# A hybrid attention block without the fifteen matrix products on a tile of ones ahead of its first data

## The chip, the cores and the metric

The kernel runs on one core of one Trainium2 chip. A core has a matrix engine (TensorE, PE in the profile, with its weight loads listed as PEld), a vector engine (VectorE, DVE), a scalar engine (ScalarE, ACT), GpSimd (POOL) and SyncE (SP), which here issues most of the DMAs. Each engine takes its own instructions in the order in which the program lists them, and waits for the others by semaphores. TensorE writes its results into PSUM, in banks of 512 float32 columns; the other operands lie in SBUF. The metric is the time of one execution on the device, in microseconds (us).

## The reference

The reference is one layer of a trunk with three groups of attention heads, on 512 tokens of width 1024, in float32. Cut to what matters here:

```python
hn = rms_norm(x, ln_mix)                 # per token
z  = hn @ w_in                           # 1024 x 3590, columns split among the head groups
# group A: 4 heads, difference of two softmax maps, ALiBi bias, norm per head
# group B: 6 heads, bias from a cumulative forget gate
# group C: 6 heads, clipped relative-position bias
# q and k of every head are normalised: q / sqrt(mean(q^2) + eps) * gain
h = x + concat(o_a, o_b, o_c) @ w_out
h = h + conv_gated_mlp(rms_norm(h, ln_ffn))        # width-3 causal convolution, 2816 hidden
h = h + (p @ w_ple_proj) * sigmoid(rms_norm(h, ln_ple) @ w_ple_gate)
```

The change concerns the very start: the first columns of `hn @ w_in`, the q, k and v of the first pair of group A.

## The kernel before, in words

Tokens are cut into four tiles of 128 (`NT`), the width of 1024 into eight slices of 128 (`KD`). To keep float32 accuracy at the faster matrix rate, each operand is split into a rounded high part and a low rest; a product is then three products, high by high, high by low and low by high (`mm3`). Split activations lie transposed in `Th` and `Tl`, and split weights are called `A_hi`/`A_lo`, `A_h`/`A_l` or `w_hi`/`w_lo` in the profile. ScalarE makes the high part (a cast), VectorE the low one (a subtraction).

The kernel begins with the loads. `load_k` (line 248) brings one slice of transposed x and one slice of the first weights for each of the eight slices k, nearly all on SyncE's queue; the weights of the second projection (`A0b_r`) and the four token tiles of x (`h`, by `load_x`, line 255) follow on the same queue. A few small loads go by ScalarE's and GpSimd's queues. These SyncE loads are kept in the order of the program.

Between the loads and the first products stands the part that the change touches. `wt` (line 100) is a tile of ones in a corner of `oall`, which later holds attention outputs. `warm(WARM)` (lines 269 and 297) makes 15 float32 products of 128 x 64 on it into a PSUM bank `wm` of the ring `t`, which has three banks; nothing reads the result.

`first_products` (line 299) follows. For each slice k it makes `th`, the weight split `wh`/`wl` and `tl`, and then 12 products: three combinations by four token tiles, accumulated in four PSUM banks `z0`, two from the ring `z` and two from the ring `s`. So 96 products of 128 x 384 make the first projection, and all four token tiles end together. x is not normalised before the product; the factor of each token, `rstd`, is applied afterwards. `stats` (line 293) has ScalarE square and sum each token tile of x (`n_sq`), and GpSimd makes 1/sqrt of it. Only behind these four stand, in ScalarE's order, the squares of the projection (`A_sq`), from which VectorE and GpSimd make the norm of each head (`A_rs`); then come the scaled q and k (`A_zn`) and v (`A_V`).

TensorE goes on with the second projection (`A0b_z`, three products per slice and token tile, into banks from the rings `t`, `o`, `t` and `s` for the four token tiles), with the transposes of the scaled q and k (`A_q_p`, `A_k_p`) set between them, and then with the projections of the following head pairs, among whose products the attention of the finished pairs is dealt out by a written table of slots. TensorE's order is pinned throughout; those of ScalarE and VectorE are pinned in the first projection and from the attention on. Later stages (output projection, gated MLP, gated embedding) follow a list of tasks with planned costs.

Of the kernel before, what the change touches and what calls it, by code (L numbers as in the profile page):

```python
# [15 lines left out]
P = 128  # L16
# [4 lines left out]
HD = 64  # L21
# [32 lines left out]
def kernel(ctx: ExitStack, tc: tile.TileContext, x, xt0, xt, pt_in, small, g_ffn_in, bias_c,  # L54
# [31 lines left out]
    pe, act, dve, pool, sp = (Engine(e) for e in (nc.tensor, nc.scalar, nc.vector, nc.gpsimd, nc.sync))  # L86

    def bank(tag, name):
        return ps.tile([P, 512], F32, tag=tag, bufs={"z": 2, "s": 2, "t": 3, "o": 1}[tag], name=name)
# [7 lines left out]
    ap = p1.__enter__()  # L97
    oall = ap.tile([P, 6, S], F32, tag="oall", name="oall")

    wt = oall[:, 4, P : 2 * P]  # L100
    dve.memset(wt, 1.0)
    nhalf = cp.tile([P, 8], F32, tag="nhalf", name="nhalf")
    dve.memset(nhalf, -0.5)
    onec = cp.tile([P, 1], F32, tag="onec", name="onec")
# [1 line left out]
    ident = cp.tile([P, P], F32, tag="ident", name="ident")  # L106
    make_identity(nc, ident)
    rstd = cp.tile([P, NT, 4], F32, tag="rstd", name="rstd")
    WARM = 15
    cols = cp.tile([P, 206], F32, tag="cols", name="cols")  # L110

    def col(c0, i=0):
# [151 lines left out]
    for t in range(3):  # L264
        load_x(t)
    pe.pinned = True
    wm = bank("t", "warm")

    def warm(n):
        for _ in range(n):  # L270
            pe.matmul(wm[:, 0:HD], wt, wt[:, 0:HD], start=True, stop=True)

    UP, DN = slice(0, HD), slice(HD, P)
    HALF = (UP, DN)

# [17 lines left out]
    def stats(t):  # L293
        token_stats(t, h[:, t, :], ap.tile([P, D], BF16, tag="e3", bufs=2, name=f"n1_sq{t}"))
        done("n", t)

    warm(WARM)
    z0 = [bank("zzss"[t], f"A0_z{t}") for t in range(NT)]
    def first_products():
        for k in range(KD):  # L300
# [503 lines left out]
    for j, (pr, part, *_) in enumerate(PARTS[1:], 1):  # L804
        n = w_in[j].shape[3]
# [824 lines left out]
    t = 0.0  # L1630
# [114 lines left out]
```

## Time and profile before

| | |
|---|---|
| median of 3 runs | 731.0 us (729.09 to 731.97) |
| profiled execution: span from first to last instruction | 728.0 us |
| profiled execution: total time beside the span | not given |
| TensorE busy | 709.6 us, 97% of the span |
| VectorE, ScalarE, GpSimd busy | 76%, 54%, 37% of the span |
| products on the tile of ones | from 1.04 us to the first data product at 7.47 us |

A row of a timeline gives the start in us from the beginning of the span, the length in us, the engine, the line, the operation, the tile written and the tiles read, shapes, and the number of instructions that were merged into the row. In square brackets stands the idle time of the engine just before it, and what ended that. All operations recorded through the kernel's helper carry its line, L78, so tiles tell more than lines. A float32 product appears as two records, so the 15 products on ones are 30. TensorE's matmuls overlap, so the rate is read from one start to the next, not from the length.

### The profile page before, as it was taken

The page shows a single profiled execution, that of the slowest core. Times are in us where ns is not written, and L with a number is a line of the kernel's source. Part 1 is how long each engine was busy: PE and PEld are TensorE (multiplying, and loading weights), DVE is VectorE, ACT ScalarE, POOL GpSimd, SP SyncE. Part 2 cuts the span into 40 slices and gives each one's busy share as a digit, 9 for nine tenths or more (in the row PEclk, how much of TensorE's full clock was granted, in tenths as well). Part 3 has the DMA queues.
Part 4 walks back from the last instruction along what each step waited for, and adds up shares of the span by engine and source line. Part 5 has one row for each costly group of instructions (what it writes and reads, how often), then busy time and mean ns, then how long its engine had stood idle before and what let it go on. Part 6 is the DMA issues. An engine that isn't in the chain of part 4 may idle for free. (4 is left out here: it accounts for less than half of the span.)

```text
span 728.0 us, 11909 instructions
## 1 busy us (share of the span) xinstructions
PE 709.6 (97%) x4234; PEld 637.8 (88%) x4234; DVE 555.8 (76%) x1091; ACT 393.8 (54%) x745; POOL 267.3 (37%) x355
## 2 busy tenths in 40 slices
PE   9998999999999999999999999999999999999997
PEld 9997989988999987889888899888998888899886
DVE  7678787887878854857878868787898779988552
ACT  6646775865766663554655544544445543544821
POOL 4585676766665640201201144020520004361400
PEclk9999999999999999999999999999999999999999
DMA  9453425413212125463444333562254322222441
GB/s 312 177 147 110 101 81 124 133 35 109 87 34 70 59 47 166 161 234 77 143 138 122 103 108 117 135 168 66 87 172 119 95 86 72 67 73 91 158 129 58
DMA packets 36950, 83.22 MB, mean 114 GB/s; under 512 B 4214, under 2 KB 6262, under 8 KB 36892
## 3 DMA queue, kind: packets, MB, share of 16 engines
q1 hardware_dynamic: 32844, 73.52, 31.7%
q0 software_dynamic: 3760, 8.66, 6.1%
q8 instruction: 33, 0.54, 0.3%
q10 hardware_dynamic: 288, 0.30, 0.1%
q14 instruction: 25, 0.20, 0.1%
HBM read 74.19 MB, written 4.21 MB: 108 GB/s over the span
## 5 line engine op out<-in xcount | busy, mean ns | idle before, releaser
L78 DVE TENSOR_TENSOR w_lo<-w_raw,w_hi 128x768 fp32r<-128x768 f32 (+1 forms) x118 | 113.9, 985 | 19.4 <-ACT w_hi L78 18.8
L78 ACT CAST w_hi<-w_raw 128x768 fp32r<-128x768 f32 (+1 forms) x118 | 89.6, 786 | 68.1 <-POOL w_raw L78 30.4
L78 PE MATMUL u<-Tl,w_hi 128*128 128x512 f32 (+1 forms) x336 | 125.5, 374 | 0.8 <-DVE Tl L78 0.8
L78 PE MATMUL u<-Th,w_hi 128*128 128x512 f32 (+1 forms) x336 | 125.6, 374 | 0.2 <-ACT pps L78 0.2
L78 PE MATMUL u<-Th,w_lo 128*128 128x512 f32 (+1 forms) x336 | 125.3, 373 | 0.0
L78 POOL TENSOR_TENSOR w_raw<-w_raw,w_raw 128x768 f32<-128x768 f32 (+1 forms) x30 | 54.2, 1828 | 146.9 <-DVE w_lo L78 115.4
L78 PEld LDWEIGHTS u<-Tl,w_hi 128*128 128x128 f32 x336 | 63.0, 188 | 13.0 <-DVE Tl L78 1.2
L78 PEld LDWEIGHTS u<-Th,w_hi 128*128 128x128 f32 x336 | 63.0, 188 | 12.6 <-ACT pps L78 0.7
L78 PEld LDWEIGHTS u<-Th,w_lo 128*128 128x128 f32 x336 | 63.0, 188 | 12.5
L78 DVE SCALAR_TENSOR_TENSOR c<-u,cols,c 128x511 f32<-128x511 f32 x76 | 56.7, 747 | 19.7 <-ACT c L78 18.4
L78 POOL DMA_DIRECT2D w_raw<-in_w_up_dram x9 | 7.9, 908 | 97.7 <-DMA w_raw<-in_w_up_dram 83.6
L78 ACT ACTIVATE c<-u,cols 128x512 f32<-128x512 f32 x38 | 29.5, 777 | 23.8 <-PE u L78 23.8
L78 PE MATMUL dn_X<-w_hi,g_ah 128*128 128x256 f32 x144 | 40.7, 282 | 0.3 <-DVE h L78 0.3
L78 PE MATMUL dn_X<-w_lo,g_ah 128*128 128x256 f32 x144 | 40.6, 282 | 0.3 <-DVE w_lo L78 0.3
L78 PE MATMUL dn_X<-w_hi,g_al 128*128 128x256 f32 x144 | 40.5, 281 | 0.0
L78 PE MATMUL B_z<-B_h,Th 128*128 128x384 f32 x96 | 34.5, 360 | 0.7 <-ACT B_l L78 0.7
L78 PE MATMUL C_z<-C_h,Th 128*128 128x384 f32 x96 | 34.3, 357 | 0.0
L78 PE MATMUL B_z<-B_h,Tl 128*128 128x384 f32 x96 | 32.3, 337 | 0.0
L78 PE MATMUL B_z<-B_l,Th 128*128 128x384 f32 x96 | 32.3, 337 | 0.0
L78 PE MATMUL C_z<-C_l,Th 128*128 128x384 f32 x96 | 32.3, 337 | 0.0
L78 PE MATMUL C_z<-C_h,Tl 128*128 128x384 f32 x96 | 32.3, 336 | 0.0
L78 PEld LDWEIGHTS dn_X<-w_hi,g_ah 128*128 128x128 f32 x144 | 27.1, 188 | 0.8 <-ACT w_hi L78 0.5
(484 smaller groups left out, 2153.7 us busy)
## 6 DMA issues: line engine op xcount, KB each, us to landing
w_raw<-in_w_up_dram SPq DMA_DIRECT2D x50, 384.0 KB, 3.8
w_raw<-in_w_down_dram SPq DMA_DIRECT2D x24, 384.0 KB, 3.0
w_raw<-in_w_up_dram SPq DMA_DIRECT2D x22, 256.0 KB, 3.4
B_r<-in_w_in_dram SPq DMA_DIRECT2D x12, 384.0 KB, 3.1
C_r<-in_w_in_dram SPq DMA_DIRECT2D x12, 384.0 KB, 3.3
wo_r<-in_w_out_dram SPq DMA_DIRECT2D x16, 256.0 KB, 2.9
w_raw<-in_w_ple_gate_dram SPq DMA_DIRECT2D x16, 256.0 KB, 2.9
h<-in_x_dram SPq DMA_DIRECT2D x4, 512.0 KB, 7.7
```

The source lines that it names most:

```text
L78: ins = getattr(self.eng, op)(*a, **k)
```

## The change

The tile of ones, its memset, the constant `WARM`, the PSUM bank and the 15 products are taken out. Nothing is put in their place. The first product that TensorE sees is the first on data. On every engine the remaining instructions stand in the same order as before; the tiles of the PSUM ring `t` each lie one bank further back in the ring of three.

```diff
-    wt = oall[:, 4, P : 2 * P]
-    dve.memset(wt, 1.0)
     nhalf = cp.tile([P, 8], F32, tag="nhalf", name="nhalf")
...
-    WARM = 15
...
     pe.pinned = True
-    wm = bank("t", "warm")
-
-    def warm(n):
-        for _ in range(n):
-            pe.matmul(wm[:, 0:HD], wt, wt[:, 0:HD], start=True, stop=True)
-
     UP, DN = slice(0, HD), slice(HD, P)
...
-    warm(WARM)
     z0 = [bank("zzss"[t], f"A0_z{t}") for t in range(NT)]
     def first_products():
```

## The prediction

> **What bounds the kernel now.** I read the page's busy shares first, then the chain that ended last, then TensorE's waits, then the timeline of the first 47 us. The chain, followed back from the end, stops long before it reaches the start, so it prices nothing here; the start has to be followed forward, row by row, until the engines are tied together.
>
> ```profile
> span 728.0 us, 11909 instructions
> ...
> PE 709.6 (97%) x4234; PEld 637.8 (88%) x4234; DVE 555.8 (76%) x1091; ACT 393.8 (54%) x745; POOL 267.3 (37%) x355
> ...
> PEclk9999999999999999999999999999999999999999
> ```
>
> TensorE is busy nearly all of the span, so a shift of its start can move the end, if nothing else holds the next stage back. The clock row shows full speed in every slice. The timeline of TensorE does not, and I go by its rates:
>
> ```profile
> 1.04 6.67 PE L78 MATMUL warm<-oall 128*128 128x64 f32 x30 [1.04 <-DVE onec L78]
> 7.47 1.63 PE L78 MATMUL A_z<-A_hi,Th 128*128 128x384 f32 x4
> 8.89 1.48 PE L78 MATMUL A_z<-A_lo,Th 128*128 128x384 f32 x4
> 10.18 1.48 PE L78 MATMUL A_z<-A_hi,Tl 128*128 128x384 f32 x4
> 11.46 1.07 PE L78 MATMUL A_z<-A_hi,Th 128*128 128x384 f32 x4
> 12.36 0.86 PE L78 MATMUL A_z<-A_lo,Th 128*128 128x384 f32 x4
> 13.05 0.86 PE L78 MATMUL A_z<-A_hi,Tl 128*128 128x384 f32 x4
> ...
> 25.54 0.86 PE L78 MATMUL A_z<-A_hi,Tl 128*128 128x384 f32 x4
> 26.23 0.28 PE L78 MATMUL A0b_z<-A0b_h,Th 128*128 128x262 f32 x1
> ```
>
> Columns are start, length, engine, line, operation, tiles, shapes and count. The 15 products on ones (two records each) hold TensorE from 1.04 to the first product on data at 7.47. Four data products take 10.18 - 8.89 = 1.29 us at first (0.322 each) and (26.23 - 12.36) / 20 rows = 0.69 later (0.173 each). The row at 11.46 takes 0.90 to the next, between the two, which puts the change of rate at about 11.9. So the array ran at a little over half speed until 4.4 us after dense data work began, and 10.9 us after the first product on ones: in this execution those 15 had not bought full rate by the time data work started.
>
> **When data is there.**
>
> ```profile
> 0.82 0.17 DVE L78 MEMSET oall<- 128x128 f32 x1 [0.82 <-PEq L1729]
> ...
> 3.65 0.98 DVE L78 TENSOR_SCALAR Th<-h 128x256 fp32r<-128x256 f32 x2 [2.09 <-DMA h<-in_xt_dram]
> ...
> 3.83 0.51 ACT L78 CAST A_hi<-waq 128x384 fp32r<-128x384 f32 x1 [0.38 <-DMA waq<-in_w_in_dram]
> ...
> 4.54 0.55 DVE L78 TENSOR_TENSOR A_lo<-waq,A_hi 128x384 fp32r<-128x384 f32 x1
> ...
> 5.01 0.74 DVE L78 SCALAR_TENSOR_TENSOR Tl<-h,Th 128x512 fp32r<-128x512 f32 x1
> ...
> 10.13 0.51 ACT L78 CAST A_hi<-waq 128x384 fp32r<-128x384 f32 x1 [2.59 <-DMA waq<-in_w_in_dram]
> ```
>
> The first two products need half of Th (about 4.14) and A_hi (4.34); the next two need the other half (4.63). A_lo is there at 5.09, Tl at 5.75.
>
> **The change, part by part.**
>
> The 15 products go. The first data product can start just behind 4.34; with a wake-up and a first weight load I take 4.5. Head start: 7.47 - 4.5 = 3.0 us. From there the work is dense: at 0.322 each, four products take 1.29, so A_lo is wanted at 5.8 and Tl at 7.1, both there by then. If full rate comes 4.4 us after the dense start again, it comes at 8.9. The fourth of the eight input slices, whose weight split waited for its transfer until 10.13, is wanted only when three slices of 12 products are done: 14 are done by 8.9, and 22 more at 0.173 bring that to about 12.8. So supply never empties, and the 96 products end 3.0 us earlier, near 23.3 in place of 26.2.
>
> Each microsecond that the change of rate comes later relative to the dense start costs 1 - 0.173/0.322 = 0.46 us of that, each one earlier gives as much.
>
> The memset of the ones goes: 0.17 us on VectorE, whose next data work then waited 2.09 us for a transfer. Nothing; without that cover it would be at most 0.17. The PSUM bank goes: its ring of three serves the same tiles in the same order, moved on by one buffer, and each still waits for the third before it. Nothing. The order of instructions on every engine, and of the DMA issues, is otherwise unchanged.
>
> **What is late next.** The first products feed the squares of the projection (A_sq), on ScalarE, and that engine has other work ahead of them in its order:
>
> ```profile
> 22.63 1.06 ACT L78 ACTIVATE n_sq<-h 128x1024 bf16<-128x1024 f32 x1 [1.00 <-DMA h<-in_x_dram]
> ...
> 23.93 1.06 ACT L78 ACTIVATE n_sq<-h 128x1024 bf16<-128x1024 f32 x1
> ...
> 24.90 0.18 ACT L78 ACTIVATION_READ_ACCUMULATOR n_sq<-h 128x1 f32 x1
> ...
> 25.91 0.66 ACT L78 ACTIVATE A_sq<-A_z 128x256 f32<-128x256 f32 x2 [0.82 <-PE A_z L78]
> ...
> 26.09 0.26 POOL L205 TENSOR_SCALAR rstd<-rstd 128x1 f32<-128x1 f32 x1
> ...
> 26.32 0.42 DVE L78 TENSOR_REDUCE A_rs<-A_sq 128x4 f32<-128x256 f32 x1 [6.30 <-ACT A_sq L78]
> ...
> 27.16 2.01 POOL L383 TENSOR_TENSOR A_rs<-A_rs,nhalf 128x4 f32<-128x4 f32 x2 [0.81 <-DVE A_rs L78]
> ```
>
> ScalarE takes the sums of squares of the tokens (n_sq) first. They wait for x to arrive, not for TensorE, and end at 25.08. Only then come the A_sq, which today wait 0.82 us for TensorE. That 0.82 is all that this chain can gain: of a head start of 3.0 us, 2.2 run into ScalarE's queue. GpSimd's own work behind the same sums ends at 26.35, which is 0.81 ahead of 27.16, so the next link moves by the same amount.
>
> Does TensorE need this chain, or could it keep its lead?
>
> ```profile
> 31.47 0.48 DVE L78 SCALAR_TENSOR_TENSOR A_zn<-A_z,rstd,A_rs 128x256 f32<-128x256 f32 x1
> 31.87 0.86 DVE L78 SCALAR_TENSOR_TENSOR A_V<-A_z,rstd,A_V 128x128 fp32r<-128x128 f32 x3
> ...
> 33.18 0.60 PE L78 MATMUL A_q_p<-ident,A_zn 128*128 128x128 f32 x4
> 33.54 0.37 PE L78 MATMUL A0b_z<-A0b_h,Th 128*128 128x262 f32 x1
> ...
> 39.24 0.62 ACT L78 CAST A1b_h<-A1b_r 128x512 fp32r<-128x512 f32 x1 [1.40 <-DMA A1b_r<-in_w_in_dram]
> ...
> 42.02 0.97 POOL L142 DMA_DIRECT2D A1b_l<-A1b_r  x1 [0.90 <-DVE A1b_l L78]
> 43.06 3.00 POOL L383 TENSOR_TENSOR A0b_rs<-A0b_rs,nhalf 128x4 f32<-128x4 f32 x3
> ...
> 46.09 0.48 DVE L78 SCALAR_TENSOR_TENSOR A0b_zn<-A0b_z,rstd,A0b_rs 128x256 f32<-128x256 f32 x1 [0.17 <-POOL A0b_rs L383]
> ...
> 46.63 0.33 PE L78 MATMUL A_q_p<-ident,A0b_zn 128*128 128x128 f32 x1 [0.54 <-DVE A0b_zn L78]
> ```
>
> It needs it three times. (1) The transposes at 33.18 would be reached at 30.2, but their last A_zn ends at 31.95 - 0.82 = 31.13: a new wait of 0.9. (2) The fourth A0b unit at 33.54 takes the PSUM bank that the third A_V frees, at 32.73 - 0.82 = 31.91; TensorE is there at 31.5: another 0.4. Its lead is now 33.54 - 31.95 = 1.6. (3) At 46.63 it waits for A0b_zn today. That tile hangs on three GpSimd powers from 43.06, behind a GpSimd DMA that waits for a split of the A1b weights; their loads take raw buffers that VectorE frees after the A_V. All of this is the chain that gained 0.82, so the wait grows from 0.54 to about 1.3 and the lead that leaves this point is 0.8. Behind it every engine's work hangs on TensorE or this chain, so I carry 0.8 to the end at face value.
>
> Sum: 728.0 - 0.8 = 727.2 for the span. The page gives no total beside the span; it lies 3.0 under the runs' median of 731.0, and I take those 3.0 as unchanged. **Forecast: 731.0 - 0.8 = 730.2 us.**
>
> The price of the rate change in the timed runs is not shown. Its bounds: with full rate at 7.47 already, today's 96 products would end at 7.47 + 96 x 0.173 = 24.1 and ScalarE would be the limit both before and after (gain 0). If it came 2 us later than in this trace, today would end 0.9 later and the gain would be 1.7. I take the trace's own value, the only one measured; the ends stay in the range.
>
> [...]
>
> **Rivals.**
>
> *The products on ones do open the rate in most timed runs.* For it: the three timed runs lie 2.9 us apart, so something in them varies, and the moment of full rate could be it. Against: the rate in this trace. Then the products end by about 24.1 both ways, ScalarE's 25.08 rules, and the time stays 731.0. [...]
>
> *The whole head start is carried through* to 731.0 - 3.0 = 728.0. For it: TensorE is 97% busy and waits little. It needs A_zn and A0b_zn not to be held by the sums of squares; the rows at 25.91 and 46.63 speak against.
>
> *Slower: the full rate needs a long stretch of any activity*, products on ones included. Today it came 10.9 us after the first of these. After the change activity starts at 4.5; the same 10.9 gives 15.4, when 34 products are done and 62 remain, ending at 26.1: today's 26.2 again. From there each further microsecond costs 0.46. If 14 us are needed, the projection ends at 4.5 + 14 + (96 - 43) x 0.173 = 27.7, and the time is 731.0 + 1.4 = 732.4. The far end, no full rate in this stage at all, is 4.5 + 96 x 0.322 = 35.4, some 740; the 4.4 us from dense start to full rate in this trace make that unlikely. It decides from 15.7 us on.
>
> **How the numbers follow.** A difference under 0.5% (3.7 us) is about what a measurement of this kernel can tell from none. Forecast (gain near 0.8) 0.55; no change 0.14; whole head start 0.14; slower by the late rate 0.13, of which a third beyond 734.7; 0.04 left for stalls that shift to another place. The range 728.0 to 732.4 takes in all but the last and the far end. Faster by over 0.5% needs more than the whole head start: 0.06, from run-to-run spread on that case. Slower by over 0.5%: 0.06. Within 0.5%: 0.88.
>
> **What the profile of the changed kernel would show.** First A_z product at about 4.5; rows of four 1.29 us apart, then 0.69, changing near 8.9. No idle time in front of A_sq on ScalarE, which starts at 25.1. New TensorE waits of 0.9 on A_zn near 30, 0.4 at the fourth A0b unit, and some 1.3 on A0b_zn near 45.8. A span of 727.2. I am wrong if the rate changes after 15, if A_sq starts well before 25, or if TensorE's lead at A0b_zn is not near 0.8.

## The result and the profile after

The changed kernel takes 726.2 us against 729.9 for the kernel before, measured beside it: a ratio of 0.9952, 95% interval 0.9936 to 0.9967. A second measurement gave 0.9954 (0.9939 to 0.9970). The forecast was 730.2 us, that is 0.8 us gained, with a range from 728.0. By the medians that is 3.7 us gained, and 2.9 in the second measurement (726.25 against 729.15); by the ratios it is 3.5 and 3.4, and their intervals reach from 2.2 to 4.7. So the gain is about the whole head start of 3.0, four times the forecast; whether it is more than the head start can't be told. The direction was right, the size was not.

The page of the changed kernel's profile:

```profile
span 723.4 us, 11848 instructions
...
PE 703.0 (97%) x4204; PEld 631.1 (87%) x4204; DVE 555.8 (77%) x1090; ACT 393.9 (54%) x745; POOL 265.8 (37%) x355
```

TensorE's 30 records fewer and 6.6 us less busy time are the products on ones. The timeline of TensorE, changed kernel:

```profile
4.45 1.65 PE L78 MATMUL A_z<-A_hi,Th 128*128 128x384 f32 x4 [4.45 <-ACT A_hi L78]
5.90 1.48 PE L78 MATMUL A_z<-A_lo,Th 128*128 128x384 f32 x4
7.18 1.48 PE L78 MATMUL A_z<-A_hi,Tl 128*128 128x384 f32 x4
8.46 0.97 PE L78 MATMUL A_z<-A_hi,Th 128*128 128x384 f32 x4
9.26 0.86 PE L78 MATMUL A_z<-A_lo,Th 128*128 128x384 f32 x4
...
23.13 0.28 PE L78 MATMUL A0b_z<-A0b_h,Th 128*128 128x262 f32 x1
...
30.09 0.60 PE L78 MATMUL A_q_p<-ident,A_zn 128*128 128x128 f32 x4
...
42.89 0.81 PE L78 MATMUL A_q_p<-ident,A0b_zn 128*128 128x128 f32 x4
```

In this profile the first stage went as drawn up: data products from 4.45, half rate (rows of four 1.28 us apart, 0.69 later) until about 8.7, the first projection done at 23.1 in place of 26.2. But the waits that were to eat the lead are not there. The A_q_p at 30.09 and at 42.89 start with no wait; in the kernel before they stood at 33.18 and, on A0b_zn, ended with a wait at 46.63. The lead is still 3.1 at the first of them. ScalarE shows why:

```profile
20.91 1.06 ACT L78 ACTIVATE n_sq<-h 128x1024 bf16<-128x1024 f32 x1 [0.18 <-DMA h<-in_x_dram]
...
22.19 1.06 ACT L78 ACTIVATE n_sq<-h 128x1024 bf16<-128x1024 f32 x1
...
23.25 0.64 ACT L78 ACTIVATE A_sq<-A_z 128x256 f32<-128x256 f32 x2
...
35.78 0.62 ACT L78 CAST A1b_h<-A1b_r 128x512 fp32r<-128x512 f32 x1 [0.31 <-DMA A1b_r<-in_w_in_dram]
```

The last sum of squares of x starts at 22.19 and not at 23.93, so A_sq starts at 23.25, ahead of the 25.1 that was taken for its floor; and the wait of 1.40 us for A1b_r is down to 0.31. Two transfers that no edit touches came earlier. Why they did was the question for the experiments.

### The profile page after: what moved, and what is told of

Read it like the earlier page. It is cut to its first block, busy times and chain, and to the rows that moved or that the text cites. A ratio compares the mean times of both kernels' runs of the same rounds, so it can differ in the third digit from the quotient of the medians.

```text
span 723.4 us, 11848 instructions
## 1 busy us (share of the span) xinstructions
PE 703.0 (97%) x4204; PEld 631.1 (87%) x4204; DVE 555.8 (77%) x1090; ACT 393.9 (54%) x745; POOL 265.8 (37%) x355
```

## The experiments

**Both kernels once more.** No edit; the first question was whether the arrival of x merely varies.

> The kernel before, unchanged, to see how much the arrival of x and the time vary with no change at all. Theory A (the late arrival of x in the first profile, n_sq ending at 25.08 us, is how this kernel always runs, and taking the products away is what made it 23.3): n_sq ends at 25.0 to 25.2 again, A_sq starts at 25.9. Theory B (the arrival varies from one execution to the next, whatever the kernel): n_sq ends anywhere from 23 to 25, and the ratio to before is 1.000 +- 0.001.

> The changed kernel, unchanged. Theory A: n_sq ends near 23.3 again. Theory B: n_sq ends anywhere from 23 to 25, and the ratio lies at 0.995 to 0.997, since the products on data still start at 4.45 and the mean of the x arrivals bounds the gain only now and then.

The kernel before came to a ratio of 1.0001 (0.9987 to 1.0014); its last n_sq started at 22.98 this time. The changed kernel had it at 22.51. ScalarE in the second profile of the kernel before:

```profile
22.98 1.06 ACT L78 ACTIVATE n_sq<-h 128x1024 bf16<-128x1024 f32 x1 [0.27 <-DMA h<-in_x_dram]
...
26.22 0.66 ACT L78 ACTIVATE A_sq<-A_z 128x256 f32<-128x256 f32 x2 [2.08 <-PE A_z L78]
...
39.57 0.62 ACT L78 CAST A1b_h<-A1b_r 128x512 fp32r<-128x512 f32 x1 [1.40 <-DMA A1b_r<-in_w_in_dram]
```

So x does vary: with no edit at all, A_sq here waited 2.08 us for TensorE and not 0.82. The wait for A1b_r does not: it is again 1.40 us, and in the second profile of the changed kernel no single one is over 0.42. Theory A was wrong on the 25.1. Theory B's figures held, for the end of n_sq and for both ratios, but a mere variation of x leaves the shorter wait for A1b_r without a cause. The moment of full rate varies too: 4.4 and 5.1 us after the first data product in the two profiles of the kernel before, 4.2 and 5.8 in those of the changed one, where the first projection ended at 23.1 and at 24.0. Between the second profiles the last of the A_q_p on A0b_zn moved from 46.96 to 44.21, 2.75 us, and the span by 3.2.

**Six and twenty-four products in place of fifteen.**

```diff
-    WARM = 15
+    WARM = 6        # and, in another kernel, 24
```

> 6 products on ones in place of 15: they end at 1.04 + 6 x 0.43 = 3.6 us, before data is there, so the head start is the same as in the changed kernel. If the head start alone counts: first data product at 4.45, full rate 4.0 to 4.4 us behind it, ratio as for the changed kernel (0.995 to 0.997). If the products on ones bring the full rate forward in part: full rate earlier than 8.5 us, and a ratio below that by up to 0.002. If they put it off: above.

> 24 products on ones: first data product at 7.47 + 9 x 0.43 = 11.3 us. If every microsecond by which the first data product moves is carried to the end: 3.8 us more than before, ratio 1.0053. If ScalarE's sums of squares hid part of a head start in the kernel before, nothing is hidden on this side and it is 1.0053 too, while the changed kernel gains less than its 3.0. If the products on ones open the full rate once they have run for 10.9 us: the data products run at 0.173 us from the first on, 4.4 x 0.46 = 2.0 us come back, and the ratio is 1.0025.

Six products end before data is there, so the head start is nearly whole. Yet the ratio was 0.9989 (0.9978 to 1.0000), about a quarter of the changed kernel's gain (by the interval, none of it to nearly half). ScalarE and, in the last row, TensorE, with six products:

```profile
22.02 1.06 ACT L78 ACTIVATE n_sq<-h 128x1024 bf16<-128x1024 f32 x1 [0.72 <-DMA h<-in_x_dram]
23.30 1.06 ACT L78 ACTIVATE n_sq<-h 128x1024 bf16<-128x1024 f32 x1
...
24.36 0.64 ACT L78 ACTIVATE A_sq<-A_z 128x256 f32<-128x256 f32 x2
...
39.80 0.62 ACT L78 CAST A1b_h<-A1b_r 128x512 fp32r<-128x512 f32 x1 [1.54 <-DMA A1b_r<-in_w_in_dram]
...
45.88 0.33 PE L78 MATMUL A_q_p<-ident,A0b_zn 128*128 128x128 f32 x1 [0.65 <-DVE A0b_zn L78]
```

This is the prediction's picture: n_sq holds A_sq, A1b_r is late, TensorE waits at A0b_zn, and its lead of 2.7 at the first data product is 0.75 there (46.63 less 45.88). Six products thus behave as the forecast said that none would. Nothing in TensorE's first stage explains the difference from none: with six products it ends at 23.03, in the changed kernel at 23.13.

With twenty-four the ratio was 1.0037 (1.0024 to 1.0049), between the two expectations. TensorE, with twenty-four products:

```profile
1.05 10.50 PE L78 MATMUL warm<-oall 128*128 128x64 f32 x48 [1.05 <-DVE onec L78]
11.31 1.63 PE L78 MATMUL A_z<-A_hi,Th 128*128 128x384 f32 x4
12.73 1.48 PE L78 MATMUL A_z<-A_lo,Th 128*128 128x384 f32 x4
14.01 1.40 PE L78 MATMUL A_z<-A_hi,Tl 128*128 128x384 f32 x4
15.25 0.87 PE L78 MATMUL A_z<-A_hi,Th 128*128 128x384 f32 x4
```

After 10 us of products on ones the data still starts at half rate (rows of four 1.24 to 1.42 us apart), for 3.8 us. A full rate that comes 10.9 us after any activity is out: the row at 14.01, 13.0 us after the first product on ones, still takes 1.24. So is, in this profile, a full rate brought about by these products. The time lost is less than the 3.84 us of later start; where the rest came back was not followed up.

**What six have that none have: instructions.** The DMA view lists a queue of its own for instructions. From the pages, the same row for the kernel before and after:

```profile
q8 instruction: 33, 0.54, 0.3%
```

33 packets, 0.54 MB: 16 KB each. That this is TensorE's stream is my reading of when the pieces come. TensorE's 4234 loads and 4234 products are an estimated 257 to a packet, and in the traces of both kernels the 33 pieces are 251 and 252 of its loads and products apart in the mean. The first piece inside the span comes when TensorE has started 187 of them in the kernel before, at 20.38 us, and 179 in the changed one, at 21.87. Eight other profiles show it in windows of two microseconds, from 16 to 18 us in one to 24 to 26 in another, and in each of these windows TensorE passes 185 to 189. The 15 products on ones are 60 instructions (30 loads and 30 products), so their removal moves every later piece of the stream to a later place in the work. Windows of two microseconds find them: in the kernel before from 19 to 21 us and from 35.5 to 37.5 us,

```profile
q8 instruction: 1, 0.02, 3.0%
```

that is one packet that holds one of the sixteen DMA engines for 0.030 x 16 x 2 = 0.96 us, the first while the tiles of x arrive, the second while A1b_r does. In the changed kernel the first lies between 21 and 23 us, with x all but there; the second at 36 to 38, when A1b_r has started 2.4 us earlier and is nearly through. The first moves beside loads that keep the engines full: 98.0% of the sixteen from 19 to 21 us in the kernel before. (The view lists a second instruction queue, q14; in the kernel before its first two pieces in the span lie at 30.5 and 40.9 us, outside both late transfers.) I call this theory F; that the head start alone counts, theory H.

**One late product.** One product on ones that waits for GpSimd's iota: data late, stream short.

```diff
-    warm(WARM)
...
     nc.gpsimd.memset(bones[HD:P, HD:P], 1.0)
+    pe.matmul(wm[:, 0:HD], wt, dist[:, 0:HD], start=True, stop=True)
```

> One product on ones, which waits for GpSimd's iota, in place of 15: the first data product stays late (near 7.25 us), but TensorE's stream has 28 pairs of weight load and product fewer. Theory H (the head start is all that the change gives): time as before, ratio 0.999 to 1.000. Theory F (TensorE's instructions arrive in pieces of 16 KB; with 15 products the first two pieces fall at 20 and 36.4 us into the transfers of x and of the A1b weights and make them late, without them they fall behind these): the pieces fall near 25 and near 39.5 us, ScalarE's wait of 1.4 us for A1b_r at 39.2 is gone or under 0.5, and the ratio is 0.998 to 0.999. [...]

The pieces came at 24 to 26 and 38 to 40 us, as said, but the ratio was 1.0001 (0.9991 to 1.0011): theory F had expected a gain here, and there is none to be measured. ScalarE, one late product:

```profile
22.14 1.06 ACT L78 ACTIVATE n_sq<-h 128x1024 bf16<-128x1024 f32 x1
...
25.53 0.66 ACT L78 ACTIVATE A_sq<-A_z 128x256 f32<-128x256 f32 x2 [2.23 <-PE A_z L78]
...
39.87 0.62 ACT L78 CAST A1b_h<-A1b_r 128x512 fp32r<-128x512 f32 x1 [0.64 <-DMA A1b_r<-in_w_in_dram]
```

x is early, and A_sq waits 2.23 us for TensorE. Early transfers are worth nothing that can be measured by themselves: the two effects don't add, each needs the other. (In its profile the last A_q_p on A0b_zn came at 45.98, 0.65 earlier than in the first profile of the kernel before. A lead of that size at this point does not show in the time.) A head start without them gives about a quarter (six products), they without a head start nothing that shows, both together the full gain.

**Three products.**

```diff
-    WARM = 15
+    WARM = 3
```

> 3 products on ones: they end at 1.04 + 3 x 0.43 = 2.3 us, so data starts as early as without any. Theory H: ratio as for the changed kernel, 0.995. Theory F: TensorE's stream is 6 pairs longer than the changed kernel's, the pieces fall 6 x 0.173 = 1.0 us and 6 x 0.12 = 0.7 us earlier than there, at 20.6 to 21.6 and at 35.9 to 36.2, the second inside the transfer of A1b_r; x or A1b_r is late by about 1 us, and the ratio lies between those of the changed kernel and of six products, 0.997.

The ratio was 0.9981 (0.9968 to 0.9994), in between, with runs from 725.7 to 730.5 us. The profile shows a good one (A_sq at 23.33, waits for A1b_r of 0.58 and 0.61). Theory H's 0.995 lies outside the interval. The spread would fit a piece on the edge of a transfer (it came between 21 and 22 us), but one profile can't show that, and it stays open. This kernel keeps the tile of ones, its memset and the PSUM bank, as do all the others with something in place of the 15 products. Five of its twelve runs (725.7 to 726.9 us) lie within those of the changed kernel (725.1 to 727.0), so these leftovers alone don't cost the 2 us by which six products are slower than none. A kernel with the leftovers and no product was not run.

**Six products, without the wait for x.**

```diff
-    WARM = 15
+    WARM = 6
...
-        token_stats(t, h[:, t, :], ...)
+        token_stats(t, oall[:, 0:2, :].rearrange("p a b -> p (a b)"), ...)
```

> Six products on ones, and ScalarE takes its four sums of squares over two slices of transposed x that are there early, not over the token tiles: the factors of the tokens are those of other data, all else is computed as before; x is still loaded. If ScalarE's wait for x holds the first projection's results back in the kernel with six products: A_sq starts when TensorE has them, near 23 us in place of 24.4, and the ratio falls from 0.9989 by up to 0.002. If x holds nothing: 0.999 again.

0.9973 (0.9963 to 0.9982), 1.2 us better than six products with the wait by the ratios, though the two intervals just touch; A_sq started at 22.28 in place of 24.36. So n_sq did hold the chain there, as the prediction had it. The wait for A1b_r stayed (1.23 us); that the remainder hangs on it is likely, but no run took that wait away alone.

**Short pairs: instructions without work.** The decisive pair of kernels. `WARM` is 12 or 30. In place of the 15 products stand 12 or 30 pairs of weight load and product of the smallest kind.

```diff
+    wb = wt.bitcast(BF16)
...
-            pe.matmul(wm[:, 0:HD], wt, wt[:, 0:HD], start=True, stop=True)
+            pe.matmul(wm[0:32, 0:2], wb[:, 0:32], wb[:, 0:2], start=True, stop=True)
```

> In place of the 15 products, 12 pairs of the shortest kind (bfloat16, 32 weights, 2 columns): they end near 2 us, long before data, and bring next to no work to the array, but make TensorE's stream as long as that of the kernel with six products. Theory F (the place of the 16 KB pieces of TensorE's instructions among the transfers decides): the pieces fall near 19.6 and 35 to 36.6 us, the last sum of squares of x starts at 22.8 or later, A1b_r is late by over 1 us, ratio 0.998 to 0.999 as with six products. Rival W (six products cost time by what they do on the array or in PSUM, not by their number of instructions): ratio 0.995 to 0.996 as in the changed kernel, x and A1b_r on time.

> 30 pairs of the same short kind: as many instructions as the 15 products have, ending before 4.5 us, so data starts early and TensorE's stream is as long as before. Theory F: the first piece falls 30 x 0.173 = 5.2 us earlier than in the changed kernel, near 16.4 to 17, among the first tiles of x, the second near 33, among the first A1b_r loads; either makes its transfer late by up to 1 us, ratio 0.996 to 0.999. Rival W: 0.995 to 0.996, x and A1b_r on time.

Twelve pairs gave 0.9987 (0.9977 to 0.9998), thirty 0.9991 (0.9981 to 1.0000). TensorE (first and last row) and ScalarE with twelve pairs:

```profile
1.05 0.48 PE L78 MATMUL warm<-oall 128*32 128x2 bf16 x12 [1.05 <-DVE onec L78]
...
22.02 1.06 ACT L78 ACTIVATE n_sq<-h 128x1024 bf16<-128x1024 f32 x1 [0.74 <-DMA h<-in_x_dram]
23.30 1.06 ACT L78 ACTIVATE n_sq<-h 128x1024 bf16<-128x1024 f32 x1
24.36 0.64 ACT L78 ACTIVATE A_sq<-A_z 128x256 f32<-128x256 f32 x2
...
39.87 0.62 ACT L78 CAST A1b_h<-A1b_r 128x512 fp32r<-128x512 f32 x1 [1.58 <-DMA A1b_r<-in_w_in_dram]
...
45.95 0.33 PE L78 MATMUL A_q_p<-ident,A0b_zn 128*128 128x128 f32 x1 [0.65 <-DVE A0b_zn L78]
```

Pairs that are over 3 us before data comes reproduce the kernel with six products row by row, to 0.1 us. Rival W is out: its 0.995 to 0.996 lies outside the interval. It is not the work on the array but the number of instructions ahead that makes these kernels slower than the changed one. ScalarE with thirty pairs:

```profile
18.98 1.06 ACT L78 ACTIVATE n_sq<-h 128x1024 bf16<-128x1024 f32 x1 [1.82 <-DMA h<-in_x_dram]
...
22.88 1.06 ACT L78 ACTIVATE n_sq<-h 128x1024 bf16<-128x1024 f32 x1
...
36.49 1.28 ACT L78 CAST A1b_h<-A1b_r 128x512 fp32r<-128x512 f32 x2 [1.54 <-DMA A1b_r<-in_w_in_dram]
```

Here the pieces lie earlier, at 16 to 18 and 33 to 35 us, and the lateness has moved with them: from the third tile of x to the first (1.82 us, where this tile is waited for 0.63 to 0.67 us in the other kernels), and from the fourth load of A1b_r to the first (1.54 us). The profile is of the fastest of eleven runs (727.3, median 728.4). Over all kernels with the token tiles of x, the last n_sq starts at 22.14 to 22.51 where the first piece comes after 21 us, and at 22.85 to 23.93 where it comes before. How late a given piece makes x is not fixed: it came between 19 and 21 us in both profiles of the kernel before, and the last n_sq at 23.93 and 22.98.

**Two wide products.**

```diff
-    wt = oall[:, 4, P : 2 * P]
+    wt = oall[:, 5, 0:432]
...
-            pe.matmul(wm[:, 0:HD], wt, wt[:, 0:HD], start=True, stop=True)
+            pe.matmul(wm[:, 0:432], wt[:, 0:P], wt, start=True, stop=True)
...
-    WARM = 15
+    WARM = 2
```

> Two float32 products of 128x432 on ones, from 1.3 to about 4.5 us: as long an activity ahead of the data as the data leaves room for, with the array streaming nearly all the time, in 8 instructions. [...] If streaming on ones brings nothing: full rate at 8 to 11 us, ratio 0.995 to 0.996.

TensorE, then ScalarE, with two wide products:

```profile
1.36 3.19 PE L78 MATMUL warm<-oall 128*128 128x432 f32 x4 [1.36 <-DVE onec L78]
4.43 0.99 PE L78 MATMUL A_z<-A_hi,Th 128*128 128x384 f32 x4
5.25 0.94 PE L78 MATMUL A_z<-A_lo,Th 128*128 128x384 f32 x4
6.03 0.87 PE L78 MATMUL A_z<-A_hi,Tl 128*128 128x384 f32 x4
...
30.78 0.33 PE L78 MATMUL A_q_p<-ident,A_zn 128*128 128x128 f32 x1 [0.92 <-DVE A_zn L78]
...
32.36 1.09 PE L78 MATMUL A_k_p<-ident,A_zn 128*128 128x128 f32 x4 [0.89 <-DVE A0b_zn L78]
...
33.91 0.42 PE L78 MATMUL A0b_z<-A0b_h,Th 128*128 128x262 f32 x1
34.12 0.42 PE L78 MATMUL A0b_z<-A0b_l,Th 128*128 128x262 f32 x1
...
35.16 0.28 PE L78 MATMUL A0b_z<-A0b_h,Th 128*128 128x262 f32 x1
35.28 0.28 PE L78 MATMUL A0b_z<-A0b_l,Th 128*128 128x262 f32 x1
...
23.24 1.06 ACT L78 ACTIVATE n_sq<-h 128x1024 bf16<-128x1024 f32 x1 [0.78 <-DMA h<-in_x_dram]
24.29 0.64 ACT L78 ACTIVATE A_sq<-A_z 128x256 f32<-128x256 f32 x2
...
41.72 0.62 ACT L78 CAST A1b_h<-A1b_r 128x512 fp32r<-128x512 f32 x1 [2.51 <-DMA A1b_r<-in_w_in_dram]
```

The two wide products do bring the rate here: the first rows of four data products are 0.82 and 0.78 us apart, where half rate makes 1.28, and from 6.03 us on they are 0.69 to 0.70 apart (from about 8.7 and 10.4 on in the changed kernel). TensorE ends the first projection 1.8 us ahead of the changed kernel, and loses it: the faster products call for the next piece of instructions at 19 to 21 us again, x and A1b_r are late, and the ratio is 0.9988 (0.9978 to 0.9998). Theory F doesn't account for all of this profile. TensorE waits for A_zn and A0b_zn, busy for 1.7 of the 4 us from 28 to 32, and works at about half rate behind these waits: products of 262 columns start 0.21 to 0.22 us apart from 33.47 to 34.99, and 0.12 from 35.16 on. That the waits bring this about is not shown. If all its work from 32.36 to 35.16 ran so, that costs an estimated 1.3 us (2.8 us of work at 1 - 0.12/0.22). Up to 50 us only this one of the twelve timelines shows such a stretch, and it is of the second slowest of twelve runs (729.6, median 728.0); how many of the others have it is not known. The fastest version seen stays the change as it is.

## Why the prediction was wrong, point by point

- *Start of data, supply, half rate.* Right in the first profile: 4.45 for 4.5, rows 1.28 to 1.29 apart, the change of rate near 8.7 for 8.9, no empty supply, 23.1 for 23.3. That the change of rate came within 0.2 us of the forecast is partly luck: in the second profile it came at 10.4, and the projection ended at 24.0.
- *The ones had not brought the full rate.* Right, and 24 of them did not either: the data started at half rate after 6.4 and after 10.3 us of 128 x 64 float32 products. After 3.1 us of the two wide ones its first row took 0.82 us. What makes this difference the runs don't show.
- *Memset, PSUM bank, order.* Nothing to see of them, as said.
- *"They wait for x to arrive, not for TensorE, and end at 25.08."* The step that failed, and with it "that 0.82 is all that this chain can gain". It took a transfer's time from one trace as fixed, because no edit touches it. A_sq started at 23.25 and 23.70, which is 2.66 and 2.52 earlier than in the kernel before (25.91, 26.22). Part of this is variation (22.98 for the last n_sq in the second profile of the kernel before, against 23.93), part is the change: the 16 KB pieces take a share of the same DMA engines (3.0% from 19 to 21 us), and with 60 instructions fewer the first comes at 21.87 us, when x is all but there, and not at 20.38. How much each part gives is open.
- *"The wait grows from 0.54 to about 1.3" at A0b_zn, lead 0.8.* Failed the same way: the A1b loads were taken to shift with the chain, with their wait of 1.40. That wait goes with the place of the second piece and fell to 0.31 and 0.42. The lead there was 3.26, and 2.75 between the second profiles, where a wait of 0.32 was left. The kernel with six products, where the pieces stay, shows the step as drawn up, lead 0.75 and ratio 0.9989, which is the ratio of the forecast. The path and the queueing behind it were drawn rightly; the two arrival times put into it were not constants.
- *The lead at A0b_zn is carried to the end at face value.* A further 0.45 us (second profiles) or 1.4 us (first profiles) came in later stages. Product by product, the lead between the second profiles is 2.8 us at 142 us of the kernel before, 3.3 at 210 and 3.2 at the end. The two profiles of the kernel before shift against each other by 0.95 us between 142 and 387 us, so this remainder is within what varies with no edit.
- *The 3.0 us beside the span, taken as unchanged.* The profiled run of the changed kernel took 1.7 us more than its span (725.1 against 723.4), so the rest of the 3.0 was probably the distance from the profiled run to the median. It stands on both sides of the forecast and did not move the gain.
- *Rivals.* The whole head start (0.14, 728.0 us) was nearest, but for a reason that it did not name. It also stood against a median of 731.0 that later lay at 729.9 and 729.2. The chance of 0.88 for a change of under 0.5% held by little, with 0.48% and 0.46%, and not for the reason given.

Not shown: how the packet's 0.96 us delays a load. The runs show that the lateness follows the piece, and not by which queue rule. Most of the readings are of one profile to a kernel.

## What to carry to other kernels

Removing or adding instructions moved the places at which TensorE's code is brought in here (the first piece from 16 to 18 us with thirty pairs to 24 to 26 with one late product), and the first two pieces each occupied a DMA engine for 0.96 us in the kernel before; beside loads that kept the engines 98.0% and 85.2% busy, that decided waits far from the edit. Before pricing a head start by a transfer that "does not change", look for instruction packets in the window of that transfer, and in more than one profile. A cheap test is a few of the shortest instructions: work stays, the stream moves.

## What was not expected of the hardware

Twelve pairs of 32 weights and 2 columns, 0.5 us of an otherwise idle TensorE, cost 2.0 to 2.5 us of a kernel of 726 (728.25 against 726.2; ratios 0.9987 and 0.9952), by their place in the stream and not by their work. And 10 us of float32 products of 64 columns left the array at half rate for another 3.8 us, where after 3 us of 432 columns the first row of four data products took 0.82 us (1.42 after the 10).
